# Full 128x128 products for a head pair in the delta rule and in the attention of a hybrid decoder layer

## The chip, the core and the metric

The kernel runs on one core of a Trainium2 chip. The metric is device microseconds from launch to end; three runs give the median. Engines are named as the profile names them: PE is TensorE's matmul stream and PEld its weight loads, DVE is VectorE, ACT is ScalarE, POOL is GpSimd, SP is SyncE, which here only issues transfers.

## What is computed

One decoder layer over 2048 tokens plus 16 meta tokens, float32 throughout: a norm, one input projection of 1024 to 4640 columns, two token mixers side by side, a gated merge with an output projection, and a SwiGLU block. The mixers are sliding-window attention (8 query heads, 2 key heads of 64, window 128, the meta tokens as global keys) and RWKV-7, a delta rule on a 64x64 state for each of 8 heads:

```python
def step(S, inp):
    r_t, w_t, k_t, v_t, a_t, b_t = inp
    sa = jnp.einsum('bhvk,bhk->bhv', S, a_t)
    S = S * w_t[:, :, None, :] + sa[..., None] * b_t[:, :, None, :] + v_t[..., None] * k_t[:, :, None, :]
    y = jnp.einsum('bhvk,bhk->bhv', S, r_t)
    return S, y
...
out = (jnp.einsum('bhgnqm,bmhd->bnqhgd', p_meta, v_meta)
       + jnp.einsum('bhgnqk,bnkhd->bnqhgd', p_band, v_band))
```

## The kernel before

Two threads of work share the core. The dense thread streams the weights for blocks of 512 tokens; each float32 operand is split into two parts and a product takes three passes of 128x512 (`mm3`, hi by hi, hi by lo, lo by hi). `chunk` brings 128x1024 weights from DRAM; ACT makes the hi part, DVE the lo part (`wh_`, `wl_`, six buffers of the tag `wsp`). Phase a of the four blocks is the input projection, phase c the branch products, output projection and FFN.

The mixer thread is made of generators. `rwkv(i, j)` (lines 593 to 850) handles head pair j over 256 tokens, four chunks of 64: 32 such units and one for the meta tokens. `attn(ti)` (from line 903) handles 128 queries: 16 of these. Each `yield` ends a step; `tick` (line 1008) lets a unit go on by a step after some 4 us of dense products, attention, the oldest unit and the others in turns. So between two steps of a unit PE has dense work, and DVE and ACT have that time for what the unit needs next. PE's order is that of the code (class `InOrder`); the order on DVE and ACT is set by the scheduler, with dense work at high priority.

Inside `rwkv` the loop over chunks (lines 795 to 826) has three steps. I call them A, B and C:

- **A**: `ar` x state into `ch` (one product of 128x128), then `gt[h]` x `uv`, a product of 64 columns for each of the two heads. ACT copies the right-hand side out as `rh`.
- **B**: the inverse `tt` x `rh`, two products of 64x64; DVE scales the result into `uv` (line 810).
- **C**: `gt[h]` x `uv` for the output rows and `bt` x `uv` for the new state, two products of 64 columns each; DVE updates the state `sd` (line 823), ACT copies the output rows into `yt` (line 825).

`ch` is one bank of PSUM, from a pool of two (`psc`); the other mixer products use three banks of the tag `pg` (`psg`), the dense products three of `pd`. A float32 product shows as two MATMUL records, two passes; a transpose as one.

Before the loop a unit forms `pa` (the in-context rate, one product with 64 rows, line 639), `pg` (the products inside the chunks, 8 products with 64 rows, line 723), the inverses of 32x32 blocks on POOL by way of DRAM, `pb` and `pvv` (token-major b, k and v, lines 750 to 760, `pvv` as products of 64 columns), and `pq`, twice 8 products of 32x32 (lines 775 to 790). In `attn`, for each of two groups, `py` takes the transposed scores of the own and the other tile of keys times the values (two products of 64 columns and 512 wide, line 991) and four products of 64x64 for the meta tokens (line 993).

Of the kernel before, what the change touches and what calls it, by code (L numbers as in the profile page):

```python
# [17 lines left out]
F32 = mybir.dt.float32  # L18
# [7 lines left out]
P = 128  # L26
# [12 lines left out]
LORA0 = 6                # projection chunks: 0-3 q, 4 k, 5 v, 6-8 lora, 9+3j.. r, k, v of a head pair  # L39
# [37 lines left out]
def layer(ctx, tc, x, meta, w_in, w_br, w_o, w_gate, w_up, w_down, w2a, a2, g2, vecs, sinks, gfin,  # L77
# [4 lines left out]
    class InOrder:  # L82
        """TensorE's work is issued in the order in which it is written here."""
# [29 lines left out]
    psg = pool("psg", bufs=3, space=PSUM)  # L113
    psc = pool("psc", bufs=2, space=PSUM)
# [4 lines left out]
    # ---- scratch in DRAM  # L119
# [6 lines left out]
    # ---- constants  # L126
# [15 lines left out]
    # low-rank weights in parts: rows (hi | lo); hi and lo of the first 128 rows; (hi | hi | lo | lo) of the last 32  # L142
# [46 lines left out]
    class High:  # L189
        """The dense thread's work on the vector engines goes first: TensorE waits for it."""  # L190
# [54 lines left out]
    class Acts:  # L245
        """Feature-major hi/lo parts of token-major rows (two halves of the columns each), times a gain;
        made ahead of their use."""
# [5 lines left out]
        def make(self, n=1):  # L253
            """The next n tiles; the last rows to be finished are transposed last."""
# [20 lines left out]
    # ---- meta tokens: their normed rows, feature-major, float32  # L275
    um = cp.tile([P, KT, 2, NM], F32R, name="um")
# [16 lines left out]
    def meta_chunk(ci, w):  # L293
        """The meta tokens' projections: rows hi and lo of a product, then their sum, feature-major."""
# [143 lines left out]
    def phase_c(b):  # L438
# [52 lines left out]
        # the first products wait for the norm: the next weights are split behind it  # L491
# [39 lines left out]
    # ================================================================ mixer thread: RWKV-7  # L531
# [3 lines left out]

    def shift(o, src, w, mi):
# [632 lines left out]
```

## Time and profile before

| | |
|---|---|
| runs | 3481.27 us median (3477.99 to 3482.14) |
| profiled execution | span 3476.7 us; the page gives no other time of its own |
| PE busy | 3397.3 us, 98% of the span, 17999 records |
| DVE / ACT / POOL busy | 55% / 42% / 29% |
| PE clock | 9 or more tenths in all 40 slices |
| DMA | 118 GB/s in the mean |

PE is busy nearly all the time, so the time is that of PE's list of passes and of its pauses. In the timeline, rows that follow each other and are alike are merged; the first column is the start in us, the second the time from the start of the first to the end of the last. Ends of passes are modelled and overlap, so costs are read from starts. Dense products come in threes (two with `wh_`, one with `wl_`), and the start of one `wl_` row to that of the next is the time of a three plus whatever stands between.

### The profile page before, as it was taken

Reading aid. Unit: us, or ns where it says so; the run is one execution under the profiler, and the core shown is the slowest. Engines: PE = TensorE matmul, PEld = TensorE weight load, DVE = VectorE, ACT = ScalarE, POOL = GpSimd, SP = SyncE. Lnnn points to the kernel's source line nnn. Section 1 sums busy time; section 2 is a strip of 40 time slices with the busy share of each in tenths; the row PEclk is TensorE's granted clock in tenths of the full one; section 3 lists DMA queues with packets and bytes.
Section 4 is the critical chain, followed back from the end, with each engine's and each line's share of the span. In section 5 each row is a group of like instructions: output and inputs, shape, how many; then the busy total and the mean of one; then the engine's idle time right before and its main releaser. Section 6 shows DMA issues by size and latency. Waiting matters only on the chain. (4 is left out here: it accounts for less than half of the span.)

```text
span 3476.7 us, 49797 instructions
## 1 busy us (share of the span) xinstructions
PE 3397.3 (98%) x17999; PEld 2663.6 (77%) x17999; DVE 1927.4 (55%) x3835; ACT 1461.6 (42%) x2885; POOL 1021.1 (29%) x2312
## 2 busy tenths in 40 slices
PE   8999999999999999999999999999989999999999
PEld 6877777777777777777777777777777777778887
DVE  3344445444434775656667655656666555664555
ACT  4355545454544454434443533434353332332222
POOL 0033332333333444333333234433333332100000
PEclk9999999999999999999999999999999999999999
DMA  4444444444543433332335333334533332532332
GB/s 149 152 138 134 150 140 128 127 153 128 160 127 118 152 99 111 95 95 84 92 119 170 93 95 96 99 89 136 154 93 89 95 90 87 186 97 97 97 97 97
DMA packets 228756, 409.62 MB, mean 118 GB/s; under 512 B 59789, under 2 KB 122829, under 8 KB 228510
## 3 DMA queue, kind: packets, MB, share of 16 engines
q1 hardware_dynamic: 196158, 359.13, 34.8%
q10 hardware_dynamic: 32352, 47.31, 3.8%
q8 instruction: 142, 2.33, 0.3%
q14 instruction: 104, 0.85, 0.1%
HBM read 346.29 MB, written 60.04 MB: 117 GB/s over the span
## 5 line engine op out<-in xcount | busy, mean ns | idle before, releaser
L91 PE MATMUL pi<-act_u,wh_in 128*128 128x512 f32 x2368 | 760.4, 402 | 3.9 <-DVE act_u L200 2.9
L745 POOL TENSOR_TENSOR pr<-xv,lt 128x124 f32<-128x124 f32 (+30 forms) x992 | 386.0, 389 | 589.9 <-DMA lt<-lt_d 310.7
L91 PEld LDWEIGHTS pi<-act_u,wh_in 128*128 128x128 f32 x2368 | 423.2, 189 | 92.5 <-DVE act_u L200 5.2
L91 PE MATMUL pi<-act_u,wl_in 128*128 128x512 f32 x1184 | 464.8, 393 | 0.0
L91 PE MATMUL pg<-act_f,wh_g 128*128 128x512 f32 x1408 | 451.9, 402 | 7.1 <-DVE act_f L200 7.1
L91 PE MATMUL pu<-act_f,wh_u 128*128 128x512 f32 x1408 | 446.6, 398 | 0.0
L91 PE MATMUL ph_d<-wh_d,mg_g 128*128 128x512 f32 x1280 | 425.3, 397 | 5.5 <-DVE h L200 5.5
L747 POOL TENSOR_TENSOR xv<-xv,pr 128x124 f32<-128x124 f32 (+30 forms) x992 | 388.4, 392 | 73.9
L91 PEld LDWEIGHTS pg<-act_f,wh_g 128*128 128x128 f32 x1408 | 255.5, 189 | 62.3 <-DVE act_f L200 9.8
L200 DVE TENSOR_TENSOR wl_in<-wr_in,wh_in 128x1024 fp32r<-128x1024 f32 x148 | 185.0, 1250 | 209.4 <-ACT wh_in L200 204.1
L91 PEld LDWEIGHTS pu<-act_f,wh_u 128*128 128x128 f32 x1408 | 257.5, 189 | 54.9 <-issue 1.2
L91 PEld LDWEIGHTS ph_d<-wh_d,mg_g 128*128 128x128 f32 x1280 | 240.2, 188 | 60.6 <-DVE h L200 6.7
L91 PE MATMUL pg<-act_f,wl_g 128*128 128x512 f32 x704 | 276.3, 393 | 0.0
L91 PE MATMUL pu<-act_f,wl_u 128*128 128x512 f32 x704 | 275.5, 391 | 0.0
L200 DVE SCALAR_TENSOR_TENSOR h<-ph_d,h 128x512 f32<-128x512 f32 x320 | 217.4, 686 | 86.7 <-PE ph_d L91 84.1
L91 PEld LDWEIGHTS pi<-act_u,wl_in 128*128 128x128 f32 x1184 | 222.8, 188 | 48.9
L839 POOL TENSOR_TENSOR gst<-gst,mhalf 128x4 f32<-128x4 f32 x32 | 36.0, 1127 | 756.7 <-DVE gst L838 728.4
L91 PE MATMUL ph_d<-wl_d,mg_g 128*128 128x512 f32 x640 | 249.8, 390 | 0.0
L200 ACT ACTIVATE wh_in<-wr_in 128x1024 fp32r<-128x1024 f32 x148 | 156.3, 1056 | 151.9 <-PE pi L91 138.7
L200 ACT ACTIVATE wh_g<-wr_g 128x1024 fp32r<-128x1024 f32 x88 | 93.3, 1060 | 218.0 <-PE ph_d L91 100.5
L200 DVE TENSOR_TENSOR wl_u<-wr_u,wh_u 128x1024 fp32r<-128x1024 f32 x88 | 109.1, 1239 | 118.7 <-ACT wh_u L200 118.6
L91 PE MATMUL pb<-ya,wh_br 128*128 128x512 f32 x512 | 163.6, 401 | 1.3 <-DVE h L200 1.2
(342 smaller groups left out, 5795.8 us busy)
## 6 DMA issues: line engine op xcount, KB each, us to landing
wr_in<-in_w_in SPq DMA_DIRECT2D x148, 512.0 KB
wr_g<-in_w_gate SPq DMA_DIRECT2D x88, 512.0 KB
wr_u<-in_w_up SPq DMA_DIRECT2D x88, 512.0 KB
wr_d<-in_w_down SPq DMA_DIRECT2D x80, 512.0 KB
proj_d<-po ACTq DMA_DIRECT2D x84, 256.0 KB
gate_d<-po ACTq DMA_DIRECT2D x64, 256.0 KB
lt<-lt_d SPq DMA_DIRECT2D x32, 512.0 KB
wr_br<-in_w_br SPq DMA_DIRECT2D x32, 512.0 KB
```

The source lines that it names most:

```text
L91: r = f(*p, **k)
L200: return f(*p, **k)
L745: G.tensor_mul(pr[:, :, :n_], xv[:, :, r:r + 1].to_broadcast([P, 4, n_]), lt[:, r, r + 1:].unsqueeze(1).to_broadcast([P, 4, n_]))
L747: G.tensor_add(xv[:, :, r + 1:], xv[:, :, r + 1:], pr[:, :, :n_])
L839: G.tensor_tensor(st[:, 3], st[:, 2], mhalf[:, 0:4], op=ALU.pow)
```

## The change

All mixer products are laid out with 128 rows and 128 columns. The two heads of a pair share one product: one operand is a block-diagonal tile whose off-diagonal blocks are zeros, written once at the start and kept (`bkd`, `vds`, `td`, `rd`).

- **pg**: `bkd` (b, then k, block-diagonal) x `ar` for each chunk, 8 products of 128x128. The masks go with it: `gb` for b, `gk` for k.
- **A**: `gk` x `vd` and `ar` x state, both summed into `see`. **B**: `td` x `rd` into `un`; DVE scales `un` into `ud`; then `bt` of k x `vd` into `new`. **C**: `bt` of b x `ud` is added to `new`; DVE makes the state; then `gb` x `ud` is added to `see`. `see`, `un` and `new` are three column ranges of the same bank `ch`.
- `psc` has one bank in place of two, `psg` four in place of three.
- `bt` is twice as large (8 transposes in place of 4, in two steps), `pvv` becomes 2 transposes, `pa` takes `dl` with 128 rows, the `yield` ahead of the loop over chunks goes, `td` comes in 4 transfers in place of 2.
- **Attention**: values stand in zero-padded tiles `vz0`, `vz1`; both groups add into one bank `py`: four products of 128 columns and 512 wide, and one for the meta tokens with a masked `ptm` that DVE makes. The four 64x64 products of each group go.
- To make room, `wsp` has five buffers in place of six, and `um` moves to another pool.

The core of the diff (comments, which go too, left out):

```diff
-    psg = pool("psg", bufs=3, space=PSUM)
-    psc = pool("psc", bufs=2, space=PSUM)
+    psg = pool("psg", bufs=4, space=PSUM)
+    psc = pool("psc", bufs=1, space=PSUM)
...
-        hi, lo = (dn.tile([P, D], F32R, tag="wsp", bufs=6, name=f"w{q}_{name}") for q in "hl")
+        hi, lo = (dn.tile([P, D], F32R, tag="wsp", bufs=5, name=f"w{q}_{name}") for q in "hl")
...
+    bkd = cp.tile([P, 2, 4, P], F32, name="bkd")
+    vds = [cp.tile([P, 4, P], F32, name=f"vd{q}") for q in range(2)]
+    td = cp.tile([P, 4, P], F32, name="td")
+    rd = cp.tile([P, P], F32, name="rd")
+    ud = cp.tile([P, P], F32, name="ud")
+    for t in (bkd, *vds, td, rd):
+        G.memset(t, 0.0)
...
-            T.matmul(pa[:, :TU], a2s[0:64, j * P:(j + 1) * P], dl[0:64], start=False, stop=True)
+            T.matmul(pa[:, :TU], a2s[:, j * P:(j + 1) * P], dl, start=False, stop=True)
...
-                T.matmul(pg[:, c * P:c * P + nr], bk[hb, c], ar[hb, c] if not m else ar[hb, c, 0], start=True, stop=True)
+                T.matmul(pg[:, c * P:(c + 1) * P], bkd[:, x, c], ar[:, c], start=True, stop=True)
...
-            T.matmul(pvv[64:128, c * P:(c + 1) * P], vm[:, c * CH:(c + 1) * CH], ident, start=True, stop=True)
+        for t in range(2):
+            T.transpose(pvv[:, t * P:(t + 1) * P], vm[:, t * P:(t + 1) * P], ident)
...
-        yield
         for c in range(n):
             s = sd[c if m else j]
             ch = psc.tile([P, 512], F32, tag="ch", name=f"ch_{nm}_{c}")
-            T.matmul(ch[:nr, 0:P], ar[:, c] if not m else ar[:, c, 0], s, start=True, stop=True)
+            see, un, new = (ch[:, k * P:(k + 1) * P] for k in range(3))
+            more = dict(start=False, stop=True, skip_group_check=True)
+            T.matmul(see, gk[:, c].rearrange("p q t -> p (q t)"), vd[:, c], start=True, stop=True)
+            T.matmul(see, ar[:, c].rearrange("p q t -> p (q t)"), s, **more)
             for h in range(2):
-                hc = slice(64 * h, 64 * h + 64)
-                T.matmul(ch[0:64, hc], gt[h][:, c, 0], uv[:, c, hc], start=False, stop=True, skip_group_check=True)
-            rh = mx.tile([64, P], F32, tag="rh", bufs=1, name=f"rh_{nm}_{c}")
-            A.activation(rh, ch[0:64, 0:P], AF.Copy)
+                hb = slice(64 * h, 64 * h + 64)
+                A.activation(rd[hb, hb], see[0:64, hb], AF.Copy)
...
             yield
-            for h in range(2):
-                hc = slice(64 * h, 64 * h + 64)
-                T.matmul(ch[0:64, P + 64 * h:P + 64 * h + 64], tt[:, h, c], rh[:, hc], start=True, stop=True)
-            V.tensor_mul(uv[0:64, c].rearrange("p (h v) -> p h v", h=2),
-                         ch[0:64, P:2 * P].rearrange("p (h v) -> p h v", h=2),
-                         rnb[:, c].unsqueeze(2).to_broadcast([64, 2, 64]))
+            T.matmul(un, td[:, c], rd, **more)
+            V.tensor_scalar(ud, un, rnb[:, c:c + 1], None, op0=ALU.mult)
+            T.matmul(new, bt[:, 1, c], vd[:, c], **more)
             yield
+            T.matmul(new, bt[:, 0, c], ud, **more)
+            V.scalar_tensor_tensor(s, new, fc[:, c:c + 1], sf, op0=ALU.mult, op1=ALU.add)
             if not m:
-                for h in range(2):
-                    hc = slice(64 * h, 64 * h + 64)
-                    T.matmul(ch[64:128, hc], gt[h][:, c, 1], uv[:, c, hc], start=False, stop=True, skip_group_check=True)
-            for h in range(2):
-                hc = slice(64 * h, 64 * h + 64)
-                T.matmul(ch[hc, 256:320], bt[:, c, hc], uv[:, c, hc], start=True, stop=True)
-            for h in range(2):
-                hc = slice(64 * h, 64 * h + 64)
-                V.scalar_tensor_tensor(s[hc, hc], ch[hc, 256:320], fc[hc, c:c + 1], sf[hc, hc], op0=ALU.mult, op1=ALU.add)
-            if not m:
-                A.activation(yt[64 * (c % 2):64 * (c % 2) + 64, c // 2], ch[64:128, 0:P], AF.Copy)
+                T.matmul(see, gb[:, c].rearrange("p q t -> p (q t)"), ud, **more)
+                A.activation(yt[64 * (c % 2):64 * (c % 2) + 64, c // 2], see[64:128], AF.Copy)
             yield
...
-                T.matmul(py[gb], vv[:, gb], pt, start=n_ == 0, stop=n_ == len(todo) - 1)
-            for j in range(4):
-                T.matmul(py[gb, j * P:(j + 1) * P], vm_t[:, j, gb], ptm, start=False, stop=True, skip_group_check=True)
-            A.activation(q[gb], py[gb].rearrange("p (j t) -> p j t", t=P), AF.Copy)
+                T.matmul(py, vv[:, g:g + 2].rearrange("p g d -> p (g d)"), pt, start=g == n_ == 0, stop=False)
+        T.matmul(py, vm_t, ptm.rearrange("p j t -> p (j t)"), start=False, stop=True)
+        A.activation(q, py.rearrange("p (j t) -> p j t", t=P), AF.Copy)
```

The order of instructions, with the engine whose semaphore each one waits for in brackets. First PE at step B of the second chunk of one unit, in the second half of a block's FFN; `pu` is a dense product. Before:

```order
L91 MATMUL pu_11_21517<-act_f_1_19416,wh_u_11_21513 128x512 x2
L91 MATMUL pu_11_21517<-act_f_1_19416,wl_u_11_21514 128x512
L91 MATMUL ch_1_1_21491<-rh_1_1_21495,tt_1_21014 64x64 [waits Activation_49]
L91 MATMUL ch_1_1_21491<-rh_1_1_21495,tt_1_21014 64x64
L91 MATMUL pu_11_21517<-act_f_2_19419,wh_u_11_21513 128x512 x2
L91 MATMUL pu_11_21517<-act_f_2_19419,wl_u_11_21514 128x512
```

The same place now:

```order
L93 MATMUL pu_11_21189<-act_f_1_19103,wh_u_11_21185 128x512 x2
L93 MATMUL pu_11_21189<-act_f_1_19103,wl_u_11_21186 128x512
L93 MATMUL ch_1_1_21164<-rd,td 128x128 [waits Activation_49]
L93 MATMUL ch_1_1_21164<-vd_117,bt_1_20351 128x128 [waits DVE_49]
L93 MATMUL pu_11_21189<-act_f_2_19106,wh_u_11_21185 128x512 x2
L93 MATMUL pu_11_21189<-act_f_2_19106,wl_u_11_21186 128x512
```

The two 64x64 products became one of 128x128, and behind it stands the product for `new`, with a wait for DVE between the two.

Then PE at step C of the same chunk, now; `ph_d` is the next dense product:

```order
L93 MATMUL pu_11_21189<-act_f_7_19174,wh_u_11_21185 128x512 x2
L93 MATMUL pu_11_21189<-act_f_7_19174,wl_u_11_21186 128x512
L93 MATMUL ch_1_1_21164<-ud,bt_1_20351 128x128
L93 MATMUL ch_1_1_21164<-ud,g_1_0_20212 128x128 [waits DVE_49]
L93 MATMUL ph_d_11_0_0_21234<-wh_d_11_0_21230,mg_g_8_20651 128x512
```

Before, the four products of this step had one wait, ahead of the first; now there is one between the two.

And DVE around the same two steps, now; `ud` (L828) and `sd` (L832) are the instructions between the products of B and of C:

```order
L202 TENSOR_TENSOR mg_g_10_21142<-th_10_21138,mg_g_10_21142 128x512 [waits Activation_49]
L202 TENSOR_TENSOR wl_d_11_0_21231<-wr_d_11_0_21228,wh_d_11_0_21230 128x1024 [waits DMAHW3_49,PE_49]
L202 SCALAR_TENSOR_TENSOR th_11_21221<-th_11_21221,pg_11_21151 128x512 [waits Activation_49]
L828 TENSOR_SCALAR ud<-ch_1_1_21164,rnb_1_19984 128x128 [waits PE_49]
L551 SCALAR_TENSOR_TENSOR rkv_3_21272<-rp_3_21273,vec,rkv_3_21272 128x256 [waits Activation_49] x3
L202 TENSOR_TENSOR wl_d_11_1_21279<-wr_d_11_1_21276,wh_d_11_1_21278 128x1024 [waits DMAHW5_49,PE_49]
L202 TENSOR_TENSOR th_11_21221<-th_11_21221,pu_11_21189 128x512 [waits DVE_49,PE_49]
L832 SCALAR_TENSOR_TENSOR sd_108<-ch_1_1_21164,fc_1_20111,sf_1_1_21169 128x128 [waits PE_49]
```

Each of the two reads `ch` and waits for PE, in a queue in which dense work stands ahead of it.

## Rows read from the trace of the kernel before

**Rows 1.** The page, part 1: busy us, share of the span, records.

```profile
PE 3397.3 (98%) x17999; PEld 2663.6 (77%) x17999; DVE 1927.4 (55%) x3835; ACT 1461.6 (42%) x2885; POOL 1021.1 (29%) x2312
```

**Rows 2.** Timeline of PE, 1736 to 1783 us: steps C, A and B.

```profile
1737.26 0.39 PE L91 MATMUL pg<-act_f,wl_g 128*128 128x512 f32 x1
...
1738.64 0.40 PE L91 MATMUL pg<-act_f,wl_g 128*128 128x512 f32 x1
...
1775.62 0.39 PE L91 MATMUL pu<-act_f,wl_u 128*128 128x512 f32 x1
...
1777.10 0.39 PE L91 MATMUL pu<-act_f,wl_u 128*128 128x512 f32 x1
...
1779.84 0.39 PE L91 MATMUL pu<-act_f,wl_u 128*128 128x512 f32 x1
...
1780.52 0.39 PE L91 MATMUL pg<-act_f,wl_g 128*128 128x512 f32 x1
1780.84 0.44 PE L91 MATMUL ch<-rh,tt 64*64 64x64 f32 x4
...
1781.78 0.40 PE L91 MATMUL pg<-act_f,wl_g 128*128 128x512 f32 x1
```

**Rows 3.** Timeline of PE, 1011 to 1013 us: four transposes of 128x128 among others.

```profile
1011.43 0.60 PE L91 MATMUL pp<-cst,sm 128*128 128x128 f32 x4
1011.86 0.27 PE L91 MATMUL ppm<-cst,smm 128*64 128x128 f32 x1
```

**Rows 4.** Timeline of PE: step B with pb and pvv, and the pg products.

```profile
1676.16 0.39 PE L91 MATMUL pg<-act_f,wl_g 128*128 128x512 f32 x1
...
1679.03 0.39 PE L91 MATMUL pg<-act_f,wl_g 128*128 128x512 f32 x1
...
1753.68 1.71 PE L91 MATMUL pg<-ar,bk 64*128 64x128 f32 x16
```

**Rows 5.** Timeline of PE around the two py steps of one attention group.

```profile
1016.57 0.39 PE L91 MATMUL pi<-act_u,wl_in 128*128 128x512 f32 x1
...
1018.85 0.40 PE L91 MATMUL pi<-act_u,wl_in 128*128 128x512 f32 x1
...
1023.09 0.39 PE L91 MATMUL pi<-act_u,wl_in 128*128 128x512 f32 x1
...
1026.00 0.39 PE L91 MATMUL pi<-act_u,wl_in 128*128 128x512 f32 x1
```

**Rows 6.** Timeline, all engines: first B step of the loop, its DVE work, the last.

```profile
390.66 0.44 PE L91 MATMUL ch<-rh,tt 64*64 64x64 f32 x4
391.13 0.28 DVE L810 TENSOR_TENSOR uv<-ch,rnb 64x128 f32<-64x128 f32 x1 [0.93 <-PE ch L91]
...
2970.94 1.23 DVE L200 TENSOR_TENSOR wl_d<-wr_d,wh_d 128x1024 fp32r<-128x1024 f32 x1 [0.18 <-ACT wh_d L200]
...
2971.33 0.44 PE L91 MATMUL ch<-rh,tt 64*64 64x64 f32 x4
...
2972.68 0.28 DVE L810 TENSOR_TENSOR uv<-ch,rnb 64x128 f32<-64x128 f32 x1
```

**Rows 7.** Timeline, 2593 us: PE lets a product go once DVE is done.

```profile
2593.07 0.28 DVE L810 TENSOR_TENSOR uv<-ch,rnb 64x128 f32<-64x128 f32 x1
...
2593.39 0.37 PE L91 MATMUL ch<-uv,g 128*64 128x64 f32 x1 [7.09 <-DVE uv L810]
```

**Rows 8.** Lines L810 and L823: idle DVE before them until PE (us, times).

```profile
  PE ch L91: 90.7, 46
...
  PE ch L91: 111.4, 73
```

**Rows 9.** DVE and ACT by line: count, busy us, mean ns, idle before (releaser).

```profile
L792 DVE TENSOR_SCALAR sd<-sd,pe 128x128 f32<-128x128 f32 x32 | 9.0, 280 | 0.0
L823 DVE SCALAR_TENSOR_TENSOR sd<-ch,fc,sf 64x64 f32<-64x64 f32 x256 | 72.2, 282 | 114.2 <-PE ch L91 111.4
L668 DVE SCALAR_TENSOR_TENSOR tw<-rkv,vec,kp 128x256 f32<-128x256 f32 x32 | 15.9, 496 | 0.8
...
L825 ACT ACTIVATE yt<-ch 64x128 f32<-64x128 f32 x128 | 35.0, 274 | 162.9 <-DVE sd L823 160.3 <-PE pg L91 0.8
```

More of the change, by code (lines that the diff above doesn't have):

```diff
@@ L702, in rwkv @@
         V.tensor_mul(ar[:, :, 0], cv(kn), pe[:, :, 0:64])
-        bk = mx.tile([P, n, 2, CH], F32, tag="bk", bufs=1, name=f"bk_{nm}")
-        V.tensor_mul(bk[:, :, 0], cv(tb), pi)
-        V.tensor_mul(bk[:, :, 1], cv(kp), pi)
-        if not m:
-            V.tensor_mul(ar[:, :, 1], cv(rm), pe[:, :, 1:65])
+        for h in range(2):
+            hb = slice(64 * h, 64 * h + 64)
+            V.tensor_mul(bkd[hb, 0, :, hb], cv(tb)[hb], pi[hb])
+            V.tensor_mul(bkd[hb, 1, :, hb], cv(kp)[hb], pi[hb])
+        V.tensor_mul(ar[:, :, 1], cv(rm), pe[:, :, 1:65])
         fc = mx.tile([P, n], F32, tag="fc", bufs=4, name=f"fc_{nm}")
@@ L748, in rwkv @@
         yield
-        pb = psg.tile([P, 512], F32, tag="pg", name=f"pb_{nm}")
-        for c in range(n):
-            T.transpose(pb[:, c * P:(c + 1) * P], bk[:, c].rearrange("p q t -> p (q t)"), ident)
-        bt = mx.tile([P, n, P], F32, tag="bt", bufs=2, name=f"bt_{nm}")
-        A.activation(bt, pb.rearrange("p (c f) -> p c f", f=P), AF.Copy)
-        uv = mx.tile([P, n, P], F32, tag="uv", bufs=2, name=f"uv_{nm}")
-        V.memset(uv[0:64], 0.0)
-        pvv = psg.tile([P, 512], F32, tag="pg", name=f"pvv_{nm}")
-        for c in range(n):
-            T.matmul(pvv[64:128, c * P:(c + 1) * P], vm[:, c * CH:(c + 1) * CH], ident, start=True, stop=True)
-        A.activation(uv[64:128], pvv[64:128].rearrange("p (c f) -> p c f", f=P), AF.Copy)
+        bt = mx.tile([P, 2, n, P], F32, tag="bt", bufs=2, name=f"bt_{nm}")
+        vd = vds[(uid + m) % 2]
+        for x in range(2):
+            pb = psg.tile([P, 512], F32, tag="pg", name=f"pb_{nm}_{x}")
+            for c in range(n):
+                T.transpose(pb[:, c * P:(c + 1) * P], bkd[:, x, c], ident)
+            A.activation(bt[:, x], pb.rearrange("p (c f) -> p c f", f=P), AF.Copy)
+            if x == 0:
+                yield
+        pvv = psg.tile([P, 512], F32, tag="pg", name=f"pvv_{nm}")
+        for t in range(2):
+            T.transpose(pvv[:, t * P:(t + 1) * P], vm[:, t * P:(t + 1) * P], ident)
+        pvt = pvv[:, :2 * P].rearrange("p (t f) -> p t f", f=P)
+        for q in range(2):
+            for h in range(2):
+                hb, qb = slice(64 * h, 64 * h + 64), slice(64 * q, 64 * q + 64)
+                if q == h:
+                    V.tensor_copy(vd[hb, q::2, hb], pvt[qb, :, hb])
+                else:
+                    A.activation(vd[hb, q::2, hb], pvt[qb, :, hb], AF.Copy)
         for _ in range(WAIT_INV):
@@ L770, in rwkv @@
+        for h in range(2):
+            for q, r32 in ((0, lo[h]), (1, hi[h])):
+                m0 = (2 * q + h) * 4
+                S.dma_start(td[r32, :, r32], xt_d[uid, m0:m0 + 4].rearrange("m j i -> j m i"))
         yield
-        tq = mx.tile([CH, 8, 32], F32, tag="tl", bufs=2, name=f"tq_{nm}")
-        t11, qs = tq[0:32], tq
-        late(V.transpose(t11, tt[0:32, :, :, 0:32].rearrange("p h c i -> p (h c) i")))
+        tq = mx.tile([P, n, 32], F32, tag="tl", bufs=2, name=f"tq_{nm}")
+        for h in range(2):
+            late(V.transpose(tq[lo[h]], td[lo[h], :, lo[h]]))
@@ L774, in rwkv @@
         yield
-        pq = psg.tile([P, 512], F32, tag="pg", name=f"pq_{nm}")
+        pqs = [psg.tile([P, 512], F32, tag="pg", name=f"pq_{nm}_{h}") for h in range(2)]
         for h in range(2):
             for c in range(n):
-                e = 4 * h + c
-                T.matmul(pq[32:64, e * 32:(e + 1) * 32], gt[h][0:32, c, 0, 32:64], t11[:, e], start=True, stop=True)
-        pqv = pq[:, :256].rearrange("p (h c i) -> p h c i", c=4, i=32)
-        qsv = qs.rearrange("p (h c) i -> p h c i", c=4)
@@ L782, in rwkv @@
-        A.activation(qsv[32:64], pqv[32:64], AF.Copy)
+                T.matmul(pqs[h][hi[h], c * 32:(c + 1) * 32], gb[lo[h], c, 0, 32:64], tq[lo[h], c], start=True, stop=True)
+            A.activation(tq[hi[h]], pqs[h][hi[h], :P].rearrange("p (c i) -> p c i", i=32), AF.Copy)
         yield
-        pq = psg.tile([P, 512], F32, tag="pg", name=f"pq2_{nm}")
-        pqv = pq[:, :256].rearrange("p (h c i) -> p h c i", c=4, i=32)
+        pqs = [psg.tile([P, 512], F32, tag="pg", name=f"pq2_{nm}_{h}") for h in range(2)]
@@ L863, in set_keys @@
                 V.tensor_sub(kw[d, g, 1, cols], k[gb], f32(kw[gb, g, 0, cols]))
-    vm_t = cp.tile([4 * NM, 4, P], F32, name="vm_t")
+    vzs = [cp.tile([P, 3, 64], F32, name=f"vz{q}") for q in range(2)]
+    vm_t = cp.tile([P, P], F32, name="vm_t")
+    for t in (*vzs, vm_t):
+        G.memset(t, 0.0)
     def roped(o, src, rot, cs, w, name):
@@ L892, in attn_meta @@
         S.dma_start(vt[:, :NM], proj_d[5][:, 0:NM])
-        V.memset(vm_t, 0.0)
         yield
         yield
-        v0 = mx.tile([P, P], F32, tag="vt", bufs=2, name="v0_m")[:NM]
-        v_rows(vt, NM, "m", v0)
+        pv = psg.tile([P, 512], F32, tag="pg", name="pv_m")
+        T.transpose(pv[:NM, :P], vt[:, :NM], ident)
+        v0 = mx.tile([P, P], F32, tag="kr", bufs=1, name="v0_m")[:NM]
+        A.activation(v0, pv[:NM, :P], AF.Copy)
         for j in range(4):
-            S.dma_start(vm_t[j * NM:(j + 1) * NM, j], v0)
-    vprev = [None]
+            for g in range(2):
+                r = 2 * NM * j + NM * g
+                S.dma_start(vm_t[r:r + NM, 64 * g:64 * g + 64], v0[:, 64 * g:64 * g + 64])
     def attn(ti):
@@ L939, in attn @@
             yield
-        vc_ = mx.tile([P, P], F32, tag="vt", bufs=2, name=f"vt_{ti}")
-        v_rows(vt, P, f"{ti}", vc_)
+        pv = psg.tile([P, 512], F32, tag="pg", name=f"pv_{ti}")
+        T.transpose(pv[:, :P], vt, ident)
+        A.activation(vzs[odd][:, 0::2], pv[:, :P].rearrange("p (g d) -> p g d", g=2), AF.Copy)
+        smm = mx.tile([P, 4, 2, NM], F32, tag="kr", bufs=1, name=f"smm_{ti}")
         for g in range(2):
@@ L973, in attn @@
             yield
-            todo = [(own.start, P, vc_)]
-            if ti:
-                todo.append((other.start, P, vprev[0]))
-            for n_, (o, wd, vv) in enumerate(todo):
+            for n_, (o, vv) in enumerate([(own.start, vzs[odd]), (other.start, vzs[1 - odd])][:2 if ti else 1]):
                 pp = psg.tile([P, 512], F32, tag="pg", name=f"pp_{nm}_{o}")
```

79 lines of the change are left out of this document (37 added, 42 removed).

## Prediction

> **What bounds the kernel now.** The page's first part comes first: PE is busy 3397.3 us of a span of 3476.7 us, DVE little more than half of it [rows 1]. Whatever shortens PE's list shortens the kernel, and whatever makes PE stand lengthens it; the other engines matter only where PE waits for them. PE stands for 79 us in all, the start included. So two things have to be read: what a step of the mixers costs on PE, and how long an answer from another engine takes when PE has to wait for it. The first is in PE's timeline. Two `wl_` rows of dense work that follow each other lie 0.68 us apart (1779.84 to 1780.52); where a mixer step stands between, the rest is its price, with what it costs to go into a tile of 64 rows or columns and back [rows 2]. The second is in the timeline of all engines.
>
> **The loop over chunks, what it saves.** Step A costs 1777.10 - 1775.62 - 0.68 = 0.80 us, step B 1781.78 - 1780.52 - 0.68 = 0.58, step C 1738.64 - 1737.26 - 0.68 = 0.70 [rows 2]. After the change each of them is two products of 128x128, four passes. Four transposes of 128x128, each with weights of its own, take 0.43 us, 0.11 a pass [rows 3]. So each step is 0.44 us, though the zeros double its arithmetic: it no longer pays for entering and leaving a small tile. That saves 0.36 + 0.14 + 0.26 = 0.76 us a chunk, and 32 units have 128 chunks: 97 us. The four chunks of the meta unit are not counted.
>
> **The rest of a unit.** The step with B, `pb` and `pvv` costs 1679.03 - 1676.16 - 0.68 = 2.19 us; less B's 0.58 that is 1.61 for `pb` and `pvv` [rows 2, 4]. Now it is ten transposes, 1.10: 0.51 saved. `pg` had 16 passes in 1.71 us [rows 4] and has 16 of 0.11, 1.76: 0.05 lost. For `pa` I take 0.3 saved: A has two passes of 0.11 and four of 64 columns, about 0.055 each, together 0.44 of its 0.80, so going into a small tile and back costs about 0.36. The second `pq` now runs into step A of the first chunk and saves an exit, 0.1. Together 0.86 us a unit, times 32: 28 us.
>
> **Attention.** The step with the own keys costs 1018.85 - 1016.57 - 0.68 = 1.60 us, of which four transposes are 0.44; the one with the other keys and the meta tokens 1026.00 - 1023.09 - 0.68 = 2.23 [rows 3, 5]. A group is 3.39 us, a tile of queries 6.78. Now a tile has five products 512 wide, ten passes. No row shows such a pass with 128 columns. From below it is four times 0.11, 0.44; from above, half of the 1.16 us that two such passes take with their small tile, 0.58. I take 0.47, near the lower end, since the upper holds an entry and an exit. That is 4.7 us and saves 2.1; one transpose of `ppm` less makes it 2.2, and 15.5 tiles (the first has no other keys) make 34 us, with ends of 16 and 39. All savings together: 97 + 28 + 34 = 159 us.
>
> **What the change adds: PE stands twice a chunk.** The order shows it. In B the product for `new` waits for DVE right behind the product for `un`, in C the product `gb` x `ud` waits for DVE right behind the one for `new`, with no dense work between. PE takes its list in order, so all that follows waits too. DVE reads one range of the bank `ch` (`un` into `ud`, `new` into `sd`) and PE wants to write another. The trace of before shows that ranges of this bank are not told apart: ACT's copy `yt`, which reads the output rows of `ch`, sat idle for 160.3 us until DVE's `sd`, which reads other columns and gives it nothing [rows 9]. The Trainium skill, page "PSUM — Partial Sum Buffer", section "PSUM bank collisions raise a hardware error", says the same as a rule against this layout: two engines must not be on one bank and quadrant of partitions at a time, whichever columns they touch, so access is to be guarded by bank. By that rule the pauses below are all paid; without it the sum would be that of the first rival.
>
> **What one pause costs.** At best DVE is free. `un` is two passes, the second 0.11 us behind the first and 0.27 long by the model, as the row of `ppm` has it [rows 3], so it ends at 0.38. DVE starts 0.03 us after the end of the products (390.66 + 0.44 to 391.13) [rows 6], at 0.41 to 0.42, and takes 0.28 for 128x128 [rows 9]. PE starts 0.04 us after DVE's end (2593.35 to 2593.39) [rows 7], at about 0.75; without the wait it would have gone on at 0.22. That is 0.53. After a wait the weights have not been loaded ahead: the first pass behind one takes 0.37 us and not 0.27 [rows 3, 7], so 0.63. In C the instruction has a second tensor: 0.28 us for 64 columns and 0.50 for 256 [rows 9] put 128 columns at 0.35, hence 0.70. With 132 pauses in B (the meta unit's four too) and 128 in C that is 83 + 90 = 173 us, the lower end.
>
> Mostly DVE is not free. In B it sat idle until PE 46 times in 128, in C 73 times [rows 8]; otherwise other work stood ahead of it. In the first B step its work started 0.47 us after the first pass, in the last one 1.35, behind a weight split of 1.23 us [rows 6]; over all 128 pairs of the timeline, of which these are the first and the last, the mean is 0.82 us more than in the first. For C I scale by the counts, 0.82 x 55 / 82 = 0.55. That adds 132 x 0.82 + 128 x 0.55 = 178 us, the upper end being 351. In the order of the changed kernel dense work still stands right ahead of both (`th` ahead of `sd`), so nothing makes DVE freer. But while PE stands it hands DVE nothing new, so the longest queues should not all return. I take three quarters, 134, and 307 in all.
>
> **Small things.** Five buffers for split weights: where a block's last weights are held as two pairs, the next lo part can only be made late, one split of 1.23 us [rows 6] at eight places, 10 us (0, if the norm there hides it, to 25). ACT's second copy of `bt` and DVE's halved products lie beside dense work in steps of 4 us; if that cover goes, they only join the queue above. The `yield` that goes puts the scaling of `sd` just ahead of A; its input is long there, so I cost it at nothing. `td` takes two transfers more on SP; a step still stands between them and their use.
>
> **Sum.** 3476.7 - 159 + 307 + 10 = 3635 us for the span; the runs' median lies 4.6 us over the profiled span, so **3639 us**, 4.5% slower.
>
> **Rivals.** *The waits do not bind.* The order names the engine that a product waits for, not the instruction; it could be an older one, done long before, as with the one wait ahead of C in the order of before. Then PE never stands and the savings stay: 3481 - 159 + 10 = 3332, faster. It is decided at a pause of (159 - 10) / 260 = 0.57 us: below it the change gains. Against it speak the ACT row [rows 9] and that the best case is 0.63. I give it 0.08.
>
> *DVE answers at once.* The scheduler knows the new order and keeps DVE clear where PE needs it: only the lower end is paid, 3481 - 159 + 173 + 10 = 3505. For it: a majority of C's work found DVE idle [rows 8]. Against it: B's did not. 0.14.
>
> *Full passes are dearer than transposes.* If a float32 product of 128x128 took 0.19 us a pass and not 0.11, the 12 passes of a chunk would cost 128 x 12 x 0.08 = 123 us more, 3762. Against it: `pg` on 64 rows already streams 128 columns to 128 columns at 0.107 a pass [rows 4]. 0.06.
>
> **Numbers.** My forecast has 0.72. About 0.2%, 7 us, is what a measurement of this kernel can tell from no change. The range runs from just under the second rival to the upper ends (3481 - 141 + 351 + 25 = 3716): 3500 to 3716; what lies outside is the first rival, the third, and the second's lowest corner. Faster 0.08, all of it the first rival; same 0.02, the lowest corner of the second with the largest savings; slower 0.90.
>
> **What would show it.** Right: in the list of waits PE's `ch` stands at the top, waiting for `ud` 132 times and for `sd` 128 times, some 250 us or more; PE's busy time falls by some 160 us; the step A lies 1.12 us apart where it was 1.48; rows of 64 or 32 columns of `ch`, `py` and `pvv` are gone. Wrong: `ch` waits for DVE only a few times, or well under 0.57 us each; or A does not shrink; or PE waits for something that is not named here, such as split weights.

## The result, and the profile after

The changed kernel takes 3700.44 us (median of 4 runs, 3699.02 to 3704.58) against 3479.63 us for the kernel before on the same chip (4 runs, 3476.47 to 3482.14): 1.0639 times as long, 95% interval 1.0624 to 1.0654. The forecast was 3639 us with a range of 3500 to 3716; the time lies inside it, and the reason is the one named first: PE stands twice a chunk.

The page of the changed kernel, to be read against [rows 1]: its span, the busy times of part 1, and of part 2 the rows of PE and of its clock in tenths, over 40 slices of the span:

```profile
span 3702.7 us, 47537 instructions
PE 3345.6 (90%) x16909; PEld 2721.0 (73%) x16909; DVE 1918.3 (52%) x3796; ACT 1504.4 (41%) x3101; POOL 997.9 (27%) x2321
...
PE   8999889999889888889888899988888899999999
...
PEclk9999999999999999999999999999999999999999
```

PE has less to do (3345.6 us where it had 3397.3) and still ends 226 us later: its share falls from 98% to 90%, over the whole of the mixers' stretch. The list of waits, PE alone (us, times, longest), says for what:

```profile
PE ch L93 <- DVE ud L828: 138.3, 126, 11.0
PE ch L93 <- DVE sd L832: 132.3, 128, 6.2
PE ph_d L93 <- DVE h L202: 15.4, 7, 5.3
```

Two rows hold 270.6 us of the 348.4 that the whole list adds up to; in the kernel before the list adds up to 70.5. The timeline of PE shows both halves of the change, the shorter steps and the pauses:

```profile
3176.37 0.39 PE L93 MATMUL ph_d<-wl_d,mg_g 128*128 128x512 f32 x1
...
3177.50 0.39 PE L93 MATMUL ph_d<-wl_d,mg_g 128*128 128x512 f32 x1
...
3181.38 0.38 PE L93 MATMUL ch<-rd,td 128*128 128x128 f32 x2
3183.55 0.49 PE L93 MATMUL ch<-vd,bt 128*128 128x128 f32 x2 [1.79 <-DVE ud L828]
...
3187.77 0.39 PE L93 MATMUL pg<-act_f,wl_g 128*128 128x512 f32 x1
3187.99 0.38 PE L93 MATMUL ch<-ud,bt 128*128 128x128 f32 x2
3188.82 0.49 PE L93 MATMUL ch<-ud,g 128*128 128x128 f32 x2 [0.44 <-DVE sd L832]
3189.06 0.70 PE L93 MATMUL pg<-act_f,wh_g 128*128 128x512 f32 x2
3189.60 0.39 PE L93 MATMUL pg<-act_f,wl_g 128*128 128x512 f32 x1
```

Step A lies between the first two rows, 1.13 us apart, where [rows 2] has 1.48: four passes for 0.45. Step C, at 3187.99, has the shortest pause there is: its first product and the dense row behind it start 1.07 us apart (3187.99 to 3189.06), which would be 0.36 without a wait. So a bare pause, one in which DVE was free, is 0.71 us, though the row itself shows 0.44 of idle time: it starts to count at the end of the products, and the pass behind a wait is slow (the row of two passes takes 0.49 us and not 0.38). The B step at 3181.38 has a pause with a queue; DVE's timeline there reads:

```profile
3181.41 1.23 DVE L202 TENSOR_TENSOR wl_u<-wr_u,wh_u 128x1024 fp32r<-128x1024 f32 x1 [0.50 <-PE ph_d L93]
3182.55 0.68 DVE L202 SCALAR_TENSOR_TENSOR h<-ph_d,h 128x512 f32<-128x512 f32 x1
3183.15 0.34 DVE L828 TENSOR_SCALAR ud<-ch,rnb 128x128 f32<-128x128 f32 x1
```

A weight split begins just as the product does, a sum of the dense work follows, then comes `ud`. Over the 256 pairs of products in the loop the pause, from the start of one product to that of the other less the 0.22 us without a wait, has a median of 0.61 us in B and 0.69 in C, about half of them at the bare minimum, and means of 1.27 and 1.20; with 0.10 for the slow pass behind, they sum to 342 us.

A second loss was not in the prediction: PE's clock. First by windows (us in the window, PE, PEld, DVE, ACT and POOL busy, granted clock, DMA share, GB/s) around the longest pause, then PE's timeline there:

```profile
1890.00:1904.00 14.00, 13.55 (x63) 11.12 (x63) 6.25 (x9) 4.87 (x11) 11.41 (x34) 1.00 0.19 61
1904.00:1907.40 3.40, 0.84 (x5) 0.56 (x3) 0.00 (x0) 0.00 (x0) 0.14 (x1) 1.00 0.09 21
1907.40:1921.00 13.60, 5.19 (x13) 4.22 (x14) 6.03 (x10) 3.98 (x6) 0.00 (x0) 0.50 0.63 192
1921.00:1935.00 14.00, 13.07 (x68) 10.85 (x67) 10.66 (x21) 7.04 (x17) 0.00 (x0) 1.00 0.49 156
```

```profile
1915.81 0.80 PE L93 MATMUL ch<-vd,bt 128*128 128x128 f32 x2 [10.97 <-DVE ud L828]
...
1916.83 0.63 PE L93 MATMUL ph_d<-wl_d,mg_g 128*128 128x512 f32 x1
1917.26 1.05 PE L93 MATMUL ph_d<-wh_d,mg_g 128*128 128x512 f32 x2
```

PE stood from 1904.8 to 1915.8; within that the granted clock fell to 0.50 (1.2 of 2.4 GHz) and stayed there for 13.6 us, 5 of them with work, whose dense rows lie 0.43 us apart (1916.83 to 1917.26) and not 0.23. Over the span the mean granted clock is 0.976; before it was 0.992; the page's row in tenths, 9 in every slice, hides this. If all that is missing is time at one half, that is 178 us against 56. In the timelines 194 dense passes are followed at the slow spacing, against 61 before. So the clock's cost is estimated at 133 x 0.2 = 27 us as a lower end, and half of the 122 us more, 61, as an upper one.

### The profile page after: what moved, and what is told of

Same layout as the page of the kernel before. It is cut to its first block, busy times and chain, and to the rows that moved or that the text cites. A ratio compares the mean times of both kernels' runs of the same rounds, so it can differ in the third digit from the quotient of the medians.

```text
span 3702.7 us, 47537 instructions
## 1 busy us (share of the span) xinstructions
PE 3345.6 (90%) x16909; PEld 2721.0 (73%) x16909; DVE 1918.3 (52%) x3796; ACT 1504.4 (41%) x3101; POOL 997.9 (27%) x2321
## 5 line engine op out<-in xcount | busy, mean ns | idle before, releaser
L93 PE MATMUL pi<-act_u,wh_in 128*128 128x512 f32 x2368 | 769.9, 406 | 1.8 <-DVE act_u L202 1.6
L761 POOL TENSOR_TENSOR pr<-xv,lt 128x124 f32<-128x124 f32 (+30 forms) x992 | 371.5, 375 | 597.4 <-DMA lt<-lt_d 342.1
L93 PE MATMUL ph_d<-wh_d,mg_g 128*128 128x512 f32 x1280 | 437.8, 407 | 16.0 <-DVE h L202 15.4
L763 POOL TENSOR_TENSOR xv<-xv,pr 128x124 f32<-128x124 f32 (+30 forms) x992 | 378.5, 382 | 74.1
L93 PEld LDWEIGHTS ph_d<-wh_d,mg_g 128*128 128x128 f32 x1280 | 247.8, 194 | 70.4 <-DVE h L202 18.1
L93 PE MATMUL ch<-vd,bt 128*128 128x128 f32 x256 | 65.3, 338 | 140.9 <-DVE ud L828 138.3
L93 PE MATMUL ch<-ud,g 128*128 128x128 f32 x256 | 65.3, 338 | 132.3 <-DVE sd L832 132.3
L202 DVE TENSOR_TENSOR wl_d<-wr_d,wh_d 128x1024 fp32r<-128x1024 f32 x80 | 99.9, 1249 | 157.9 <-PE pg L93 69.6
```

Of the source, the lines that this page charges most:

```text
L93: r = f(*p, **k)
L202: return f(*p, **k)
L761: G.tensor_mul(pr[:, :, :n_], xv[:, :, r:r + 1].to_broadcast([P, 4, n_]), lt[:, r, r + 1:].unsqueeze(1).to_broadcast([P, 4, n_]))
L763: G.tensor_add(xv[:, :, r + 1:], xv[:, :, r + 1:], pr[:, :, :n_])
```

## The experiments

All twelve runs follow. The ratio behind each time compares it with the kernel before on the same chip (3473 to 3479 us). Not all kernels ran on one chip, so differences between them are given by these ratios too where it matters.

**1. Both steps reordered.** In both steps the product that DVE reads is written last, behind the one that had waited, in the same bank:

```diff
+            T.matmul(new, bt[:, 1, c], vd[:, c], **more)
             T.matmul(un, td[:, c], rd, **more)
             V.tensor_scalar(ud, un, rnb[:, c:c + 1], None, op0=ALU.mult)
-            T.matmul(new, bt[:, 1, c], vd[:, c], **more)
             yield
+            if not m:
+                T.matmul(see, gb[:, c].rearrange("p q t -> p (q t)"), ud, **more)
             T.matmul(new, bt[:, 0, c], ud, **more)
             V.scalar_tensor_tensor(s, new, fc[:, c:c + 1], sf, op0=ALU.mult, op1=ALU.add)
             if not m:
-                T.matmul(see, gb[:, c].rearrange("p q t -> p (q t)"), ud, **more)
                 A.activation(yt[64 * (c % 2):64 * (c % 2) + 64, c // 2], see[64:128], AF.Copy)
```

> In step B the product of bt k with vd is written ahead of the product of td with rd, and in step C the product of gb with ud ahead of that of bt b with ud, so that TensorE reaches the end of each step without waiting for VectorE; the tile stays in one PSUM bank and the number of products is the changed kernel's. Theory 1 (the two waits inside a step are the loss): some 348 us of pauses go and the saving of about 155 us stays, 3479.6 - 155 = 3325 us, 3300 to 3350; the waits of ch for ud and sd fall from 270 us to under 30, and the mean granted clock comes back to about 0.99. Rival (the full-size passes, the fifth wsp buffer or the fourth psg buffer cost the time): the time stays within 30 us of 3700.

Measured: 3442.72 us, 0.9886 of the kernel before (0.9866 to 0.9906). The rival is out: 258 us come back by the order of two products alone. The wait of `ch` for `sd` has left PE's list, and the one for `ud` is

```profile
PE ch L93 <- DVE ud L829: 2.8, 1, 2.8
```

But 117 us of the 375 expected did not come. Step B is now as short as A (PE's timeline: 1.13 us apart, from 1746.18 to 1747.31), and so is C (1750.74 to 1751.87):

```profile
1746.18 0.39 PE L93 MATMUL pg<-act_f,wl_g 128*128 128x512 f32 x1
1746.40 0.38 PE L93 MATMUL ch<-vd,bt 128*128 128x128 f32 x2
1746.62 0.39 PE L93 MATMUL ch<-rd,td 128*128 128x128 f32 x2
1746.76 0.71 PE L93 MATMUL pg<-act_f,wh_g 128*128 128x512 f32 x2
1747.31 0.39 PE L93 MATMUL pg<-act_f,wl_g 128*128 128x512 f32 x1
```

so the steps are not what is left. PE's waits are, 158.7 us in all:

```profile
PE ch L93 <- ACT yt L836: 37.6, 13, 5.9
PE py L93 <- ACT ptt L991: 19.5, 8, 4.9
```

and the clock, 0.980, has hardly come back, where 0.99 was expected: what is left are fewer but long stands. One of them, followed back through three timelines, of PE, ACT and SP:

```profile
2248.20 0.39 PE L93 MATMUL ph_d<-wh_d,mg_g 128*128 128x512 f32 x1
2253.27 0.49 PE L93 MATMUL ch<-vd,g 128*128 128x128 f32 x2 [4.69 <-ACT yt L836]
```

```profile
2251.87 1.06 ACT L202 ACTIVATE wh_u<-wr_u 128x1024 fp32r<-128x1024 f32 x1 [12.09 <-DMA wr_u<-in_w_up]
2252.95 0.27 ACT L836 ACTIVATE yt<-ch 64x128 f32<-64x128 f32 x1
```

```profile
2232.56 0.33 SPq L212 DMA_DIRECT2D wr_g<-in_w_gate  x1
2245.05 0.62 SPq L788 DMA_DIRECT2D xt_d<-xv  x1
...
2247.67 0.36 SPq L212 DMA_DIRECT2D wr_u<-in_w_up  x1
```

PE may not begin a new `ch` before ACT has copied `yt`; ACT takes its list in order and stands 12.09 us at a weight chunk that has not arrived; that load was issued only at 2247.67, because SP, also in order, stood from 2232.9 to 2245.05 at the transfer of an inverse that POOL was still computing. In the kernel before ACT waits far less for weight loads. The largest two of seven rows, first here (319.9 us in all), then in the kernel before (57.3 in all):

```profile
ACT wh_in L202 <- DMA wr_in<-in_w_in: 74.2, 27, 9.4
ACT wh_u L202 <- DMA wr_u<-in_w_up: 66.2, 17, 12.1
```

```profile
ACT wh_br L200 <- DMA wr_br<-in_w_br: 23.6, 4, 8.3
ACT wh_g L200 <- DMA wr_g<-in_w_gate: 17.8, 5, 6.7
```

**2. The order kept, `new` in a second bank.** The bank is taken from the small products:

```diff
-    psg = pool("psg", bufs=4, space=PSUM)
-    psc = pool("psc", bufs=1, space=PSUM)
+    psg = pool("psg", bufs=3, space=PSUM)
+    psc = pool("psc", bufs=2, space=PSUM)
...
-            see, un, new = (ch[:, k * P:(k + 1) * P] for k in range(3))
+            cn = psc.tile([P, 512], F32, tag="ch", name=f"cn_{nm}_{c}")
+            see, un, new = ch[:, 0:P], ch[:, P:2 * P], cn[:, 0:P]
...
-            T.matmul(new, bt[:, 1, c], vd[:, c], **more)
+            T.matmul(new, bt[:, 1, c], vd[:, c], start=True, stop=True)
```

> The order of the changed kernel is kept, but the k product of new goes to a tile in a second PSUM bank, for which the small-product pool goes from 4 buffers to 3. Theory 1, if the shared bank makes the wait of step B: the B pause (138 us of waits, some 180 us by starts) goes, while in step C the b product of see still shares the bank of see alone and no longer that of new, so its wait goes too: 3325 to 3360 us. Rival (VectorE's queue and not the bank makes TensorE wait): the waits of ch for ud and sd stay near 270 us and the time near 3700.

Measured: 3470.37 us, 0.9970 (0.9956 to 0.9984), 10 runs. PE's waits of `ch` for `ud` are gone and those for `sd` come to 6.0 us, with the products in the changed kernel's order: PE stands because the two products share a bank (which is here also one tile of the program), and DVE's queue only lengthens the stand. The time is 110 us over the upper end expected, the clock is 0.974, and again the list (171.2 us in all) has long waits for ACT:

```profile
PE ch L93 <- ACT yt L836: 16.7, 4, 6.6
PE py L93 <- ACT ptt L991: 16.2, 7, 5.0
...
PE pgt L93 <- ACT sig L663: 15.2, 9, 6.2
...
PE ch L93 <- DVE sd L833: 6.0, 3, 4.1
```

The wait of `pgt` is most likely the price of the bank: it needs a small-product buffer, of which three are left, and experiment 1, with four, has no such row.

**3. Only step B reordered.** The first two changed lines of experiment 1 alone: the product of `bt` k with `vd` moves, C stays.

> Only step B is reordered (k product of new ahead of the product of td with rd); step C is the changed kernel's. Theory 1: the B pause goes (some 180 us by starts) and the C pause stays (some 168 us): 3700 - 180 = 3520 us, less up to 20 us for the clock, 3490 to 3540; the wait of ch for sd stays near 130 us, that for ud falls under 20. Rival (one pause takes over what the other leaves, as VectorE is equally late in both): under 90 us is gained, 3610 or more.

Measured: 3581.79 us, 1.0289 (1.0274 to 1.0305): 119 us back, between the theory (160 to 210) and the rival (under 90). The row of PE's waits says where the rest of B's pause went:

```profile
PE ch L93 <- DVE sd L832: 174.4, 127, 7.8
```

It was 132.3 in the changed kernel: C's pause takes over 42 us of what B's leaves. That DVE's other work, which B's pause had let pass, now stands ahead of `sd` is the likeliest reason; it was not followed further.

**4. The two DVE operations at the priority of the dense work.** `V` becomes `HV` in both lines.

> Nothing but the place of two VectorE operations in its queue is changed: ud and the new state are given the priority of the dense work's operations. Theory 1a (half of the pause is VectorE's queue, half the turnaround of product, VectorE, product): the pause falls from a mean of 1.34 to the least seen, 0.72 us, so 260 x 0.62 = 160 us come back, 3540 us, 3510 to 3590; the waits of ch fall from 270 to about 130 us. Rival (the pause is the turnaround and what already runs on VectorE, which priority does not move): under 60 us, 3640 or more.

Measured: 3709.07 us, 1.0653 (1.0632 to 1.0673), with waits of 140.2 and 135.8 us. This tells nothing of the queue: all 3796 DVE records of the trace stand in the order of the changed kernel. The run is a repetition of it, 0.2% off. Whether `ud` could pass the work ahead of it was not tried in another way.

**5. Both steps reordered, two `ch` buffers and three small ones.**

```diff
-    psg = pool("psg", bufs=4, space=PSUM)
-    psc = pool("psc", bufs=1, space=PSUM)
+    psg = pool("psg", bufs=3, space=PSUM)
+    psc = pool("psc", bufs=2, space=PSUM)
```

> The reordered steps B and C of the first run with the PSUM banks shared out as in the kernel before: two buffers for ch, three for the small products. In the first run 158.7 us of TensorE's waits were left against 70.5 us in the kernel before, 37.6 of them in ch for the copy yt, which must be read before the only ch buffer is written again. Theory (the fifth bank moved from ch to the small products costs these): the wait for yt goes, 3442.7 - 38 = 3405 us, with some of the half-clock stretches 3390 to 3410. Rival (three small-product buffers, one of them held by py over both heads, make other waits, as the 15.2 us of pgt for sig in the second run): 3425 to 3450, with the waits of pgt, pg, psS and pvv up by 20 us or more.

Measured: 3447.94 us, 0.9903 (0.9884 to 0.9922): as the rival had it. The wait for `yt` is gone; waits of 15.5 us of `pgt` for `sig` and of 8.3 of `pvv` for `tl` have come. The single `ch` buffer was where ACT's lateness showed, not its cause.

**6. The attention part alone, in the kernel before.** Its functions are the changed kernel's, the recurrence and all buffers the kernel before's.

> The kernel before with the attention part of the change alone (py summed over heads and blocks in one bank, values in zero-padded tiles, one transpose and one product for the meta keys); the recurrence, the pools and their buffers are the kernel before's. Theory (the attention term of the prediction): 15.5 units by 2.2 us, 34 us less, 3445 us, 3435 to 3455. Rival (py now held over both heads takes one of three buffers, and the waits for a buffer give the gain back): 3465 to 3490, with the waits of psS, pp and pg up by 20 us or more.

Measured: 3472.77 us, 0.9983 (0.9973 to 0.9992), 10 runs: 7 us. The time is in the rival's range, but its mechanism is not there: the waits of `psS` and `pp` come to 2.9 us where they had 4.7. The step with the own keys is 1.30 us (1015.70 - 1013.72 - 0.68) where it was 1.60 [rows 5]:

```profile
1013.72 0.39 PE L91 MATMUL pi<-act_u,wl_in 128*128 128x512 f32 x1
1013.94 1.02 PE L91 MATMUL py<-ptt,vz 128*128 128x512 f32 x2
1014.80 0.60 PE L91 MATMUL pp<-cst,sm 128*128 128x128 f32 x4
...
1015.70 0.40 PE L91 MATMUL pi<-act_u,wl_in 128*128 128x512 f32 x1
```

So one 512-wide product of two passes takes 1.30 - 0.44 = 0.86 us. A tile now has 2 x 1.30 + 0.86 + 1.72 = 5.18 us where it had 2 x (1.60 + 2.23) = 7.66; with one `ppm` less that is 2.6 us by 15.5 tiles, 40 us saved on PE's list. Of these, 18 us come back as waits (88.7 us in all against 70.5; `py` for `ptt` 9.4 and `pgt` for `ta` 7.6, before 1.3 and 0.7), and up to 14 as clock (0.988 for 0.992).

**7. One step more for the inverses**, on experiment 1: `WAIT_INV = 10`.

> The first run (both steps reordered) with ten steps instead of nine left to the inverses, which gives back to a unit the step that the change had dropped between its second inverse product and its first chunk. In the first run SP's queue stood 282 us at the transfer of xv to memory, waiting for POOL's last inverse step, with weight loads queued behind it, and ScalarE waited 319.9 us for weight loads (57.3 us in the kernel before), with yt, ptt and others behind it. Theory (the late inverses hold SP's queue, that the weight loads, these ScalarE, and ScalarE TensorE): with 32 units by some 4 us more time the wait for xv falls under 190 us, ScalarE's wait for weight loads under 220 us, and the time to 3400 to 3430 us. Rival (the fifth instead of the sixth buffer of split weights makes them late): ScalarE's wait for weight loads stays over 280 us and the time within 12 us of 3443.

Measured: 3453.75 us, 0.9930 (0.9914 to 0.9945): as the rival had it. SP still stands 289.5 us at `xv` (282.0 in experiment 1), and ACT 331.4 us at weight loads; why the step more does not shorten SP's stand was not followed.

**8. Five buffers of split weights in the kernel before**, `bufs=6` to `bufs=5` for `wsp`.

> The kernel before with five instead of six buffers of split weights, the change's smallest part alone. The prediction took 10 us for it: 3489 us. Theory 2 (the sixth buffer was the slack that kept weight loads off TensorE's way): ScalarE's wait for weight loads rises from 57.3 to over 200 us as in the changed kernels, and the time to 3500 to 3540 us. Rival (nothing waits for it): 3475 to 3485 us.

Measured: 3491.08 us, 1.0040 (1.0026 to 1.0054). ACT's waits for weight loads rise to 228.9 us, as theory 2 says, but the time by only 12, near the 10 that the prediction took: PE's waits are 78.1 us for 70.5, so little of what ACT loses reaches PE there.

**9. Experiment 1 with six buffers of split weights.** The room is made in the attention:

```diff
-        hi, lo = (dn.tile([P, D], F32R, tag="wsp", bufs=5, name=f"w{q}_{name}") for q in "hl")
+        hi, lo = (dn.tile([P, D], F32R, tag="wsp", bufs=6, name=f"w{q}_{name}") for q in "hl")
...
-        cs = mx.tile([P, 2, P], F32, tag="cs", bufs=1, name=f"cs_{ti}")
+        sx = mx.tile([P, 4, 272], F32, tag="sm", bufs=1, name=f"sx_{ti}").rearrange("p j t -> p (j t)")
+        cs = sx[:, :2 * P].rearrange("p (k t) -> p k t", k=2)
...
-        kl = mx.tile([P, 1, P], F32, tag="kl", bufs=1, name=f"kl_{ti}")
+        kl = sx[:, 2 * P:3 * P].unsqueeze(1)
...
-        vt = mx.tile([P, P], F32, tag="vl", bufs=1, name=f"vl_{ti}")
+        vt = sx[:, 3 * P:4 * P]
...
-                pt = mx.tile([P, 512], F32, tag="pt", bufs=1, name=f"ptt_{nm}_{o}")
+                pt = q.rearrange("p j t -> p (j t)")
```

> The first run (both steps reordered) with the sixth buffer of split weights back; the room for it comes from the attention's staging tiles, which lie in tiles that are not in use at the time. The first run had 319.9 us of ScalarE's waits for weight loads (57.3 us before) and 158.7 us of TensorE's waits (70.5 us before). Theory (ScalarE, held at a weight load, keeps yt, ptt and the like from TensorE): ScalarE's wait for weight loads falls under 150 us, TensorE's waits to some 90 us, and the time by 12 us and up to 70 us more, 3380 to 3425 us. Rival (the sixth buffer is worth here what it was worth in the kernel before, 12 us): 3425 to 3437 us. Second rival (the shorter steps themselves leave the loads late): over 3437.

Measured: 3407.24 us, 0.9798 (0.9780 to 0.9816): in the theory's range, 36 us less than experiment 1 by the times and 31 by the ratios, though PE's waits fall only to 132.4 us, not to 90. What the attention's new tiles cost or save by themselves was not measured. ACT's waits for weight loads are 105.4 us, PE's wait for `yt` is down to 14.4, and the largest row is the dense work's own:

```profile
PE ph_d L93 <- DVE h L202: 27.4, 14, 9.6
PE ch L93 <- ACT yt L836: 14.4, 7, 3.5
PE ch L93 <- DVE ud L829: 14.2, 3, 7.8
```

**10. The same with two `ch` buffers and three small ones** (the edit of experiment 5).

> The kernel of the run above with two buffers for ch and three for the small products, the kernel before's sharing of the PSUM banks. Theory: as the two were equal in the first and the fifth kernel tried (3443 and 3448 us), within 12 us of the run above. Rival (with ScalarE on time, the one ch buffer or else the fourth small-product buffer decides): over 12 us apart.

Measured: 3435.34 us, 0.9874 (0.9859 to 0.9888), 28 us over experiment 9 on the same chip, as the rival had it. With ACT less late the changed kernel's sharing of the banks is the better one.

**11. The changed kernel, its order kept, with six buffers** (the edit of experiment 9).

> The changed kernel, its order kept, with the sixth buffer of split weights back and the attention's staging tiles in tiles not in use at the time, as in the run of 3407 us. That sizes the buffer's share in the changed kernel's loss: 12 us in the kernel before, 36 us with the steps reordered (3443 to 3407). Theory (the pauses for ud and sd are the loss and give the weight loads time): 0 to 25 us less, 3675 to 3700 us, the waits of ch for ud and sd within 25 us of 270. Rival (the late weight loads lengthen the pauses): 40 us or more less, under 3660, with those waits under 235 us.

Measured: 3652.66 us, 1.0516 (1.0495 to 1.0537): 48 us less than the changed kernel by the times and 43 by the ratios, more than the theory allows, and not by the rival's way, since the pauses stay:

```profile
PE ch L93 <- DVE ud L828: 145.2, 128, 9.6
PE ch L93 <- DVE sd L832: 121.4, 128, 6.4
```

They are 266.6 us for 270.6. ACT's waits for weight loads fall from 205.2 to 67.6 us, and PE's other waits with them, from 75.2 to 43.5 us, `ph_d` for `h` from 15.4 to 3.8 among them.

**12. Experiment 9 with the transfers of an inverse issued by POOL**, `S.dma_start` to `G.dma_start` for `xt_d` and `td`.

> The kernel of 3407 us (both steps reordered, six buffers of split weights), with the transfers of an inverse, xv to memory and from there to td, issued by POOL instead of SP. In that kernel SP's queue stood 319.3 us at the first of them until POOL had ended xv, with weight loads behind, and ScalarE still waited 105.4 us for weight loads. Theory (SP standing at xv makes the weight loads late): that wait leaves SP's list, ScalarE's wait for weight loads falls under 60 us, and the time to 3375 to 3400 us. Rival (POOL now stands for td's last reader and the inverses come later, which holds TensorE at the products with td): 3415 us or more, with waits of pq, ch for POOL, tq or td.

Measured: 3390.44 us, 0.9752 (0.9736 to 0.9769), the shortest of all: 2.5% under the kernel before and 310 us under the changed one. The time is where the theory has it, but its mechanism is not there. SP no longer stands at the transfer of `xv` to memory (319.3 us in experiment 9) but as long at the next load into `xv`, which waits until that transfer has read the tile (SP's waits):

```profile
SPq L757 <- DMA xt_d<-xv: 346.4, 31, 18.3
```

and ACT's waits for weight loads fall only to 76.4 us. What the 17 us came from stays open.

## Why the prediction was right, and where it was off

Against the profiled execution the sum was 3635 us; its span is 3702.7, 68 us more. The terms that were too small are the queue at DVE (35 us), the clock (some 42) and PE's other waits; the range held without a term for the clock, since its upper end had room in the savings (141 us there, 163 measured) and in the 25 us for the buffer. That much of it is luck.

- **The savings: right.** Chunks: 1.13 - 0.68 = 0.45 us a step gives 0.35 + 0.13 + 0.25 = 0.73 a chunk, 93 us for 97. The rest of a unit: 0.9 us by the medians of its steps in the two traces, 29 for 28. Attention: 40 for 34, as a pass 512 wide is 0.43 and not 0.47. Together, before rounding, 163 for 159. The third rival (full passes at 0.19 us) is out: a pass is 0.11.
- **The pauses: right in place and number, 35 us too small.** `ch` waits for `ud` 126 times in the loop and for `sd` 128, and for nothing else so long. Experiments 1 and 2 show that the order within the shared bank makes them; the first rival is out. The Trainium skill's rule by banks (page "PSUM — Partial Sum Buffer", section "PSUM bank collisions raise a hardware error") agrees with experiment 2 in its outcome, no wait across two banks; whether the chip, and not only the program's guards, needs the wait inside one bank no run here shows. The bare price is 0.71 us in both steps, for 0.63 and 0.70 (where the working's 0.42 + 0.28 + 0.04 is 0.74 and not 0.75): `ud` from the bank takes 0.35 us (median), not the 0.28 of the same size from elsewhere [rows 9]. That makes 260 x 0.71 = 185 us for 173. The step that was mis-sized is "while PE stands it hands DVE nothing new, so the longest queues should not all return. I take three quarters, 134": the queue is 342 - 185 = 157 us, nearly nine tenths of the 178. About half of the pauses are bare; the others stand behind splits and sums that DVE has already begun or has ahead in its list, as at 3181.41, or, as in the longest, behind a DVE that itself waits for ACT (9.48 us of the 10.97). There ACT had stood 10.74 us at `ya` for a load (`yl`) that SP issued only at 1907.23, behind the transfer of `xv` at 1904.16 at which it had stood since 1891.2: the chain followed in experiment 1 lies already in the changed kernel's longest pause.
- **The clock: left out.** It costs an estimated 27 to 61 us, and with 163, 342 and 5 us more of PE's other waits the span's 226 leave 42 for it (226 + 163 - 342 - 5). No run changes the clock alone, so this remainder is not a measurement. It is the largest omission.
- **The sixth buffer: 10 us was right for the kernel before and wrong for the changed one.** By the ratios it is worth 14 us there (12 by the times), 43 in the changed kernel (48) and 31 with the steps reordered (36); in the sum it stands among PE's other waits, 75.2 us with five buffers and 43.5 with six. The prediction looked for it at a block's last weights; experiments 8, 9 and 11 show it in ACT's list, where a weight chunk that has not arrived holds up all that is written behind it. "if that cover goes, they only join the queue above" missed that the queue can be held by a transfer.
- **PE's busy time** fell by 52 us and not by 160: a row of two passes behind a wait is longer (0.49 for 0.38 us), and so is every row at half clock (0.63 for 0.39). In experiment 12, with the same products, it is 3254.1 us, 143 less.

The savings did not reach the end whole in any kernel. Experiment 12 is 88.6 us under the kernel before by spans, with 163 off PE's list: 52 us are waits (122.4 for 70.5), and the 22 left fit the clock (0.985 for 0.992, at most some 24 us).

## What to carry to other kernels

Where a program's guards go by a whole bank or tile, as here, two products to one bank with a reader between them are one chain, whatever columns they touch: write the product that DVE reads last, or give the other one a bank of its own, and price the hand-over by starts (0.71 us here), since the wait's row shows only 0.44. When PE's list gets shorter, look at the in-order lists of the others before counting the gain: one late load holds ACT, ACT holds PE's buffer, and a buffer that was worth 14 us is worth 31 or 43. A part that saves 40 us on PE's list can be worth 7 at the end.

## What the runs showed of the hardware

The clock was lost beside single long stands, not beside the many short pauses. The clock's record of the changed kernel has 32 falls to one half while PE still has products, and beside each PE had stood in one piece for 1.35 to 11.0 us, as from 1904.8; beside 21 of them the longest stand is a wait for `ud` or `sd`, always one of 1.79 us or more and never a bare one. Not every such stand brought a fall. Taking the pauses away did not bring the clock back: the reordered kernel, with nearly all of the 260 gone but stands of some us for ACT left, has 0.980, and experiment 2, with them gone too, 0.974, for 0.976.

The kernels with a shorter list for PE lost clock as well: its mean is 0.992 in the kernel before and 0.988, 0.980 and 0.985 in experiments 6, 1 and 12, which are all faster. Each of them has more waits of PE than the kernel before (88.7, 158.7 and 122.4 us for 70.5).
